# A new layout of SBUF for a fused encoder layer on one core: operands of the large matmuls on the left stack, raw weights and rows on the right

## The chip, the cores and the metric

The kernel runs on one core of a Trainium2 chip. The metric is the device time of one execution in microseconds; for the kernel before it is the median of three runs. The profile is of one further execution, recorded by the hardware profiler.

## The reference, cut to what matters

One layer of an encoder, in float32, for 1024 tokens of width 1024, with 256 memory tokens. Its work is nearly all matrix products:

```
n    = RMSNorm(h)
proj = n @ W_in                         # 1024 x 5120: q,k,v of attention; q,k,v,gate of retention; q of memory
y_a  = dilated windowed attention (12 heads of 64, dilations 1, 4, 16, rotary)
y_r  = bidirectional retention (6 heads, chunks of 128)
y_m  = cross attention into the 256 memory tokens (4 heads of 128)
h    = h + W_out( sum_i sigmoid(n @ W_gate_i + b_i) * (y_i @ W_proj_i) )
u    = DWConv3(RMSNorm(h) @ W_up)       # 1024 x 5632
out  = RMSNorm(h + (silu(a) * b) @ W_down)   # [a | b] = u, width 2816 each
```

## The kernel before

Every large product is done in float32r with both operands split into a high and a low part, x = xh + xl, and three matmuls per block: lh.rh, lh.rl and ll.rh (`mm3`, lines 174 to 177). The order of their operands follows the first argument as the stationary tile of 128 x 128 and the second as the streamed tile of up to 512 columns; in the profile's rows (`acc<-nTh,wh`) the streamed tile stands first. `hilo` (lines 180 and 181) makes the two parts: ScalarE copies the high one, VectorE subtracts it from the source for the low one.

Weights come through `WStream`: SP's queue loads a raw block of 128 x 1024 (`wraw`, three buffers), `hilo` splits it into `wh` and `wl` (three buffers each), TensorE uses it. The order of the loads and splits is written out once, and `get` runs the loads two or more blocks ahead. The program's order sets the order on each engine; a tile's place is given to the next tile of its tag, or to a pool opened later in the same bytes, when its last reader is through.

The stages, in the order of the profile:

- 0 to 780 us: norm and transposes of x into `nTh`, `nTl` (16 tiles of 128 x 1024 in the pool `n_p`), then the projections `acc<-nT,w`, merged by hand with the attentions' own small matmuls. Their q, k, v are tiles of `qk_p` (`qk_tile`, two buffers for each name); the retention's v comes from matmuls of 256 columns whose stationary tile is nT and whose streamed tile is w.
- 780 to 1158 us: for each of three branches the gates (`accg<-nT,w`, evacuated into q, k, v tiles of `qk_p`, six ahead) and the merge `accg<-y,w` (`gemm`). The y rows are loaded into `wraw` buffers and split into `yh`, `yl`; those of k = 0 lie in a pool of their own, `y0_p`. The sum is built in `mg` and split into `mgh`, `mgl`, which take the places of nT.
- 1158 to 1254 us: the output product `pso<-w,mg`, 256 columns, stationary tile mg.
- 1254 to 1325 us: the second norm, and the operands of the up product. That product is done by a scheme with seven products of half size for eight: operands B11, B21 (pool `na_p`) and T2, T1, T3, B22, T4 (pool `nb_p`), each of four tiles for the high and four for the low part, 128 x 512.
- 1325 to 1709 us: the up product over 22 column blocks, seven groups of twelve matmuls each (`prod`), with the convolution on ScalarE and VectorE beside it. The first three column blocks run in the stage before.
- 1709 to 1932 us: the down product `ps<-w,t`, with seven half-size products again, stationary tiles `th`, `tl` made from the rows `g` just before their use.

The pools of SBUF are two stacks: a pool opened without a side lies on the left one, which grows upward, a pool with `side="right"` on the right one, which grows downward from byte 229,344 of a partition. Summed up from the sizes of the pools, the tiles that this document speaks of begin at these bytes; the last column is what the address leaves when divided by 64 (tiles of one pool are 2048 or 4096 bytes long, so it is the same for all of them):

| tiles | before: first byte (side) | remainder |
|---|---|---|
| raw weights; wh; wl | 20,032; 32,320; 44,608 (left) | 0 |
| mh, ml (memory rows, transposed) | 118,304; 126,496 (left, behind small tables) | 32 |
| x | 93,728 (left, behind small tables) | 32 |
| q, k, v of attention, gates | 139,232 to 163,808 (right) | 32 |
| nT, later mgh, mgl | 163,808 to 229,344 (right) | 32 |
| y of k = 0: yh; yl | 131,040; 135,136 (right) | 32 |
| y of k > 0; mg | 89,664 to 130,624; 56,896 (left) | 0 |
| B11; B21 | 114,240; 130,624 (left) | 0 |
| T2, T1, T3, B22, T4 | 147,424 to 229,344 (right) | 32 |
| g of the first four; th, tl | 114,240; 130,624 (left) | 0 |
| the other g | from 147,424 (right) | 32 |

Of the kernel before, what the change touches and what calls it, by code (L numbers as in the profile page):

```python
# [11 lines left out]
F32 = mybir.dt.float32  # L12
F32R = mybir.dt.float32r
# [4 lines left out]
P = 128  # L18
D = 1024
S = 1024  # L20
KT = D // P
NT = S // P
MEM = 256
# [6 lines left out]
HALF = 512  # L30
# [115 lines left out]
def encoder_block(ctx: ExitStack, tc: tile.TileContext, x, mem, vec, w_mix, w_gate, w_pa, w_pr, w_pm,  # L146
# [5 lines left out]
    def pool(name, **kw):  # L152
        kw.setdefault("bufs", 1)
        return tc.tile_pool(name=name, reuse_waits="tile", **kw)
# [28 lines left out]
    class WStream:  # L183

        def __init__(self, wp, raw_bufs=3, bufs=3):
            self.wp, self.raw_bufs, self.bufs = wp, raw_bufs, bufs
            self.loads, self.items, self.raw, self.done = [], [], [], []
            self.i = 0  # L190

# [18 lines left out]
        def _load(self):  # L210
            parts, alt = self.loads[len(self.raw)]
            n = sum(a * b for _, a, b in parts)
            if alt:
                t = self.alt.tile([P, n], F32, name="wraw2", tag="wraw2", bufs=2)
            else:
                t = self.wp.tile([P, n], F32, name="wraw", tag="wraw", bufs=self.raw_bufs)
            at = 0
            for src, a, b in parts:
                nc.sync.dma_start(t[:, at:at + a * b], src.rearrange("p a b -> p (a b)"))
                at += a * b  # L220
            self.raw.append(t)
# [59 lines left out]
        nc.vector.scalar_tensor_tensor(dstl, pt[:, :n], gain[:, k + k0:k + k0 + 1], dsth.bitcast(F32),  # L281
                                       op0=ALU.mult, op1=ALU.subtract)

    W = WStream(ctx.enter_context(pool("w_p")))
    for i, (_, _, nr, _, _) in enumerate(mixer_blocks()):
        W.plain(chunk_spec(w_mix, i, nr // P))
    order = [(1, w_pr, 6), (0, w_pa, 6), (2, w_pm, 4)]
# [15 lines left out]
    NB = DFF // P  # L303
# [73 lines left out]
    down_items()  # L377


    rn = ExitStack()  # L380
    n_p = rn.enter_context(pool("n_p", side="right"))
    nTh = [n_p.tile([P, S], F32R, name=f"nTh{k}", tag="n", bufs=16) for k in range(KT)]
    nTl = [n_p.tile([P, S], F32R, name=f"nTl{k}", tag="n", bufs=16) for k in range(KT)]

    qk_s = ExitStack()
    qk_p = qk_s.enter_context(pool("qk_p", side="right"))
    pm = ExitStack()
    psA = pm.enter_context(pool("psA", space=PS))

# [26 lines left out]
    vmr = [ck.tile([P, 2, HALF], F32R, name="vm" + t, tag="vm" + t) for t in "hl"]  # L416
    xs_ = ExitStack()
    xp = xs_.enter_context(pool("xin"))
    mt = [xp.tile([P, D], F32, name=f"mem{t}", tag="x", bufs=6) for t in range(MEM // P)]
    xt = [xp.tile([P, D], F32, name=f"x{t}", tag="x", bufs=6) for t in range(NT)]  # L420
    for t in range(2):
        nc.sync.dma_start(mt[t], mem[t * P:(t + 1) * P, :])
        if t == 0:
# [124 lines left out]
        return ev  # L548

    def qk_tile(tag, dt=F32):  # L550
        return qk_p.tile([P, S], dt, name=tag, tag=tag, bufs=2)


    def dense_ret_qk(j, st):
# [2 lines left out]
        return [q for p in zip(a, b) for q in p]  # L557

    def dense_ret_v(j, st):
        st["v"] = [qk_p.tile([P, NT, P], F32, name="v0", tag="v", bufs=2),  # L560
                   st["pool"].tile([P, NT, P], F32, name="v1", tag="v1", bufs=2)]
        box = {}

        def vpart(t2):
            if t2 == 0:
                box["w"] = (W.get(), W.get())
            ps = acc()
            for i in range(2):
                t = 2 * t2 + i
                for k in range(KT):  # L570
                    wh, wl = box["w"][k // 4]
                    mm3(ps[:, i * 256:(i + 1) * 256], nTh[k][:, t * P:(t + 1) * P], nTl[k][:, t * P:(t + 1) * P],
                        wh[:, k % 4], wl[:, k % 4], k == 0, k == KT - 1)
            for i in range(2):
                nc.scalar.copy(st["v"][i][:, 2 * t2:2 * t2 + 2, :],
                               ps.rearrange("p (a i b) -> p a i b", a=2, i=2)[:, :, i])

        return [lambda t2=t2: vpart(t2) for t2 in range(4)]
# [411 lines left out]

    def y_part(bi, k):

        r = W.wp.tile([P, S], F32, name="yraw", tag="wraw", bufs=3)
        nc.sync.dma_start(r, y_src[bi][k * P:(k + 1) * P, :])
        a, b = y_tile("yh", k), y_tile("yl", k)
        hilo(a, b, r)
        return a, b

    def y_tile(tag, k):
        if k == 0:  # L1000
            return y0_p.tile([P, S], F32R, name=tag, tag=tag)
        return y_p.tile([P, S], F32R, name=tag, tag=tag, bufs=5)


# [31 lines left out]
    bp_s.close()  # L1036

    sgs = {}
    y0_p = qk_s.enter_context(pool("y0_p", side="right"))
    ap_s = ExitStack()  # L1040
    attn_psum(ap_s, "dil", s=3, t=2, u=1)
    psb["U"] = ap_s.enter_context(pool("dilU"))
# [24 lines left out]
        return psG.tile([P, HALF], F32, name="accg", tag="accg", bufs=8)  # L1067

    gs = ExitStack()
    mg_p = gs.enter_context(pool("mg"))  # L1070
    mg = [mg_p.tile([P, S], F32, name=f"mg{c}", tag="mg", bufs=8) for c in range(KT)]
    y_p = gs.enter_context(pool("y_p"))
    def gemm(w, rh, rl):
# [40 lines left out]
            if bi != 2 and c + GA < KT:  # L1114
                run(gate_steps(bi, c + GA, sgs, accg))
    gs.close()
    qk_s.close()
    pg.close()


# [2 lines left out]
    KP = KT // 2  # L1123
    po = ExitStack()
    psO = po.enter_context(pool("psO", space=PS))
    row_p = ctx.enter_context(pool("row_p"))
    sn_p = ctx.enter_context(pool("sn_p"))
    na_s = ExitStack()
    na_p = na_s.enter_context(pool("na_p"))
    ssq = cst.tile([P, NT, 4], F32, name="ssq")  # L1130
    h_d = dram.tile([S, D], F32, name="h_d")
    g_d = dram.tile([DFF, S], F32, name="g_d")
# [10 lines left out]
    def ops(pl, name):  # L1143
        return [[pl.tile([P, HALF], F32R, name=f"{name}{q}{k}") for q in "hl"] for k in range(KP)]

    B11, B21 = ops(na_p, "b11"), ops(na_p, "b21")
    h_t = {}

    def load_h(ts):
# [194 lines left out]
        conv_q.extend(conv_steps(st["b"], st.pop("ua"), st.pop("ub")))  # L1344

    nb_s = ExitStack()
    nb_p = nb_s.enter_context(pool("nb_p", side="right"))
    T2, T1, T3, B22, T4 = (ops(nb_p, q) for q in ("t2", "t1", "t3", "b22", "t4"))
    w1 = wget()
    pre = []  # L1350
# [68 lines left out]


    NK = NB // 2
    na_s.close()
    t_p = ctx.enter_context(pool("t_p"))
    g_t = []

    def load_g(pl, n):
        for _ in range(n):
            b = len(g_t)
            g_t.append(pl.tile([P, S], F32, name=f"g{b}"))
            nc.gpsimd.dma_start(g_t[b], g_d[b * P:(b + 1) * P, :])  # L1430

    load_g(t_p, 4)
    finish_up(last, *w32, n=(3, 3, 3))
    c12(last)
    nb_s.close()
    gb_p = ctx.enter_context(pool("gb_p", side="right"))
    W.alt = gb_p
    load_g(gb_p, NB - 4 - 2)
    hr = [row(f"hr{t}") for t in range(NT)]
    for t in range(NT):  # L1440
        nc.gpsimd.dma_start(hr[t], h_d[t * P:(t + 1) * P, :])
# [1 line left out]
    nc.gpsimd.dma_start(gfin, bass.AP(tensor=g_final.tensor, offset=g_final.offset, ap=[[0, P], [1, D]]))  # L1443

    def t_op(src):
        h = t_p.tile([P, HALF], F32R, name="th", tag="th", bufs=4)
        l = t_p.tile([P, HALF], F32R, name="tl", tag="tl", bufs=4)
        hilo(h, l, src)
        return h, l

# [71 lines left out]
    for p in range(3):  # L1522
        if p < 2:
            B = [bank() for _ in range(TP)]
        for kp in range(NK):
            w = W.get()
            prep(p * NK + kp + 1)
            if p == 0 and kp == 0:
                fill(len(conv_q))
                load_g(gb_p, 2)  # L1530
            oa, ob = ready.pop((p, kp))
            end = kp == NK - 1
            for tp in range(TP):
                tile_mm(A[tp], tp, oa, w, 0, p == 0 and kp == 0, end)
            if end:
                for tp in range(TP):
                    after_a(p, tp)
            for tp in range(TP):
                tile_mm(B[tp], tp, ob, w, 1, p < 2 and kp == 0, end)
            if end:  # L1540
                for tp in range(TP):
                    after_b(p, tp)
        if p == 0:
            early = [lambda t=t: (square(t, L, 0), gain(t, L)) for t in range(TP)]
        if p == 1:
            run(early)
# [54 lines left out]
```

## Time and profile before

| | |
|---|---|
| median of 3 runs | 1934.61 us (1932.96 to 1935.24) |
| profiled execution | 1934.28 us |
| its span, first to last instruction | 1932.5 us |
| TensorE busy | 1892.1 us, 9458 matmuls |
| VectorE busy | 1142.5 us |
| ScalarE busy | 836.6 us |

A row of the timeline gives the start and the duration of an instruction; matmuls overlap, so the time that one takes from TensorE is the distance to the next one's start. A window gives the busy time of each engine with the number of its instructions, and the granted clock (1.00 is the full 2.4 GHz).

### The profile page before, as it was taken

Reading aid. Unit: us, or ns where it says so; the run is one execution under the profiler, and the core shown is the slowest. Engines: PE = TensorE matmul, PEld = TensorE weight load, DVE = VectorE, ACT = ScalarE, POOL = GpSimd, SP = SyncE. Lnnn points to the kernel's source line nnn. Section 1 sums busy time; section 2 is a strip of 40 time slices with the busy share of each in tenths; the row PEclk is TensorE's granted clock in tenths of the full one; section 3 lists DMA queues with packets and bytes.
Section 4 is the critical chain, followed back from the end, with each engine's and each line's share of the span. In section 5 each row is a group of like instructions: output and inputs, shape, how many; then the busy total and the mean of one; then the engine's idle time right before and its main releaser. Section 6 shows DMA issues by size and latency. Waiting matters only on the chain.

```text
span 1932.5 us, 24176 instructions
## 1 busy us (share of the span) xinstructions
PE 1892.1 (98%) x9458; PEld 1555.5 (80%) x9458; DVE 1142.5 (59%) x2032; ACT 836.6 (43%) x1415; POOL 79.3 (4%) x144
## 2 busy tenths in 40 slices
PE   8999999999999999999999999979999999999997
PEld 7888988887777777788888889957888888888885
DVE  7564454654548526331233074475888887899976
ACT  7364243444556547212112133543545544445444
POOL 1000010110000000000000000000000000020001
PEclk9999999999999999999999999989999999999998
DMA  7211111110011101322112025312222222287552
GB/s 258 88 44 55 44 55 34 55 62 26 23 35 53 44 20 61 109 87 90 34 60 93 22 71 203 114 55 65 77 98 77 94 81 86 75 341 256 170 169 104
DMA packets 52162, 173.35 MB, mean 90 GB/s; under 512 B 6224, under 2 KB 6352, under 8 KB 51920
## 3 DMA queue, kind: packets, MB, share of 16 engines
q1 hardware_dynamic: 39168, 129.33, 20.3%
q0 software_dynamic: 10864, 38.80, 5.1%
q10 hardware_dynamic: 2016, 3.67, 0.5%
q8 instruction: 74, 1.21, 0.3%
q14 instruction: 40, 0.33, 0.1%
HBM read 143.47 MB, written 28.31 MB: 89 GB/s over the span
## 4 chain that ended last, share of the span: by engine, by line
PE 90%; DVE 5%; ACT 3%; issue 1%; DMA 1%; POOL 0%; SPq 0%; POOLq 0%; ACTq 0%; DVEq 0%
PE ps L177 10%; PE ps L176 10%; PE ps L175 10%; PE acc L175 8%; PE acc L177 8%; PE acc L176 8%; PE accg L176 7%; PE accg L177 7%; PE accg L175 7%; PE psu L827 2%; PE pso L177 2%; PE pso L175 2%; PE pso L176 2%; PE pss L783 2%; PE pst L810 1%
## 5 line engine op out<-in xcount | busy, mean ns | idle before, releaser
L181 DVE TENSOR_TENSOR wl<-wraw,wh 128x1024 fp32r<-128x1024 f32 (+2 forms) x239 | 270.8, 1134 | 318.5 <-ACT wh L180 318.5
L180 ACT CAST wh<-wraw 128x1024 fp32r<-128x1024 f32 (+2 forms) x239 | 233.1, 980 | 403.6 <-PE accg L176 170.0
L175 PE MATMUL acc<-nTh,wh 128*128 128x512 f32 x640 | 260.0, 406 | 0.7 <-ACT v L541 0.7
L177 PE MATMUL acc<-nTh,wl 128*128 128x512 f32 x640 | 255.1, 399 | 0.0
L176 PE MATMUL acc<-nTl,wh 128*128 128x512 f32 x640 | 254.5, 398 | 0.0
L175 PEld LDWEIGHTS acc<-nTh,wh 128*128 128x128 f32 x640 | 120.5, 188 | 31.8 <-issue 4.6
L177 PEld LDWEIGHTS acc<-nTh,wl 128*128 128x128 f32 x640 | 120.5, 188 | 28.7 <-issue 1.4
L176 PEld LDWEIGHTS acc<-nTl,wh 128*128 128x128 f32 x640 | 120.7, 189 | 25.5 <-issue 0.7
L176 PE MATMUL ps<-wl,th 128*128 128x512 f32 x308 | 119.8, 389 | 0.0
L175 PE MATMUL ps<-wh,th 128*128 128x512 f32 x308 | 119.8, 389 | 0.0
L177 PE MATMUL ps<-wh,tl 128*128 128x512 f32 x308 | 119.6, 389 | 0.2 <-DVE tl L181 0.2
L177 PE MATMUL accg<-nTh,wl 128*128 128x512 f32 x288 | 114.2, 396 | 0.0
L175 PE MATMUL accg<-nTh,wh 128*128 128x512 f32 x288 | 114.2, 396 | 0.0
L176 PE MATMUL accg<-nTl,wh 128*128 128x512 f32 x288 | 114.2, 396 | 0.0
L529 ACT COPY sw<-acc 32x512 f32<-32x512 f32 x144 | 83.1, 577 | 45.8 <-PE acc L177 39.3
L176 PE MATMUL accg<-yl,wh 128*128 128x512 f32 x256 | 100.4, 392 | 0.0
L175 PE MATMUL accg<-yh,wh 128*128 128x512 f32 x256 | 99.6, 391 | 0.8 <-ACT v L985 0.8
L177 PE MATMUL accg<-yh,wl 128*128 128x512 f32 x256 | 100.3, 392 | 0.0
L180 ACT CAST th<-g 128x512 fp32r<-128x512 f32 x66 | 41.0, 620 | 86.7 <-PE ps L176 70.0
L175 PE MATMUL pso<-wh,mgh 128*128 128x256 f32 x256 | 73.1, 286 | 0.0
L177 PE MATMUL pso<-wh,mgl 128*128 128x256 f32 x256 | 72.5, 283 | 0.0
L176 PE MATMUL pso<-wl,mgh 128*128 128x256 f32 x256 | 71.9, 281 | 0.0
(364 smaller groups left out, 4150.7 us busy)
## 6 DMA issues: line engine op xcount, KB each, us to landing
wraw<-in_w_mlp_dram SPq DMA_DIRECT2D x90, 512.0 KB, 4.1
wraw<-in_w_mix_dram SPq DMA_DIRECT2D x48, 512.0 KB, 3.5
wraw<-in_w_gate_dram SPq DMA_DIRECT2D x24, 512.0 KB, 3.5
g_d<-cv POOLq DMA_DIRECT2D x22, 512.0 KB, 2.9
g<-g_d POOLq DMA_DIRECT2D x22, 512.0 KB, 13.6
wraw<-in_w_out_dram SPq DMA_DIRECT2D x16, 512.0 KB, 3.7
wraw<-in_w_mlp_dram SPq DMA_DIRECT2D x22, 256.0 KB, 3.1
x<-in_x_dram SPq DMA_DIRECT2D x8, 512.0 KB, 5.7
```

Source lines behind the costliest of these rows:

```text
L175: nc.tensor.matmul(o, lh, rh, start=first, stop=False, **kw)
L176: nc.tensor.matmul(o, lh, rl, start=False, stop=False, **kw)
L177: nc.tensor.matmul(o, ll, rh, start=False, stop=last, **kw)
L180: nc.scalar.copy(hi, src)
L181: nc.vector.tensor_sub(lo, src, hi.bitcast(F32))
L529: nc.scalar.copy(sw[q * 32:(q + 1) * 32], ps[o * 32:(o + 1) * 32])
L783: nc.tensor.matmul(ps[:, a * w:(a + 1) * w], st["q"][r, q0:q0 + P], st["k"][r, k0:k0 + w], start=True, stop=True)
L810: nc.tensor.transpose(pv[:, k, a], sm[:, a, k * P:(k + 1) * P], ident)
L827: nc.tensor.matmul(u[64 * i:64 * i + 64, c], loc["V"][:, vslot[k0 + k * P], 64 * i:64 * i + 64], pt[:, k, a], start=k == 0, stop=k == nk - 1)
```

## The change

The allocation of SBUF alone is changed; no engine instruction is added or taken away. The split weights stay on the left and raw weights get a pool `wr_p` on the right. A ring of eight tiles of 128 x 1024, `ab`, follows on the left and serves in turn memory rows and x, q, k and v of all attentions, both v of the retention, gates, y of k = 0, B11 and B21 (high and low part as two halves of one tile), the first four g and th, tl. nT comes behind it on the left, and nb_p and gb_p take its place later. mg, row_p (h, ua, ub, cv and others) and sn_p (half rows) go to the right.

| tiles | after: first byte (side) | remainder |
|---|---|---|
| wh; wl | 20,032; 32,320 (left) | 0 |
| the ring ab | 44,608 to 77,376 (left) | 0 |
| nT, later mgh, mgl | 77,376 to 142,912 (left) | 0 |
| mh, ml | from 187,936 (left, behind small tables) | 32 |
| y of k > 0 | 142,912 to 183,872 (left) | 0 |
| T2, T1, T3, B22, T4 | 77,376 to 159,296 (left) | 0 |
| the other g | from 77,376 (left) | 0 |
| raw weights | 217,056 to 229,344 (right) | 32 |
| mg; row_p; sn_p | 184,288; 167,904; 159,712 (right) | 32 |

```diff
-        def __init__(self, wp, raw_bufs=3, bufs=3):
+        def __init__(self, wp, rp, raw_bufs=3, bufs=3):
...
-                t = self.wp.tile([P, n], F32, name="wraw", tag="wraw", bufs=self.raw_bufs)
+                t = self.rp.tile([P, n], F32, name="wraw", tag="wraw", bufs=self.raw_bufs)
...
-    W = WStream(ctx.enter_context(pool("w_p")))
+    W = WStream(ctx.enter_context(pool("w_p")), ctx.enter_context(pool("wr_p", side="right")))
...
+    ab_p = ctx.enter_context(pool("ab_p"))
+
+    def ab(name, dt=F32, shape=(P, S)):
+        return ab_p.tile(list(shape), dt, name=name, tag="ab", bufs=8)
+
     rn = ExitStack()
-    n_p = rn.enter_context(pool("n_p", side="right"))
+    n_p = rn.enter_context(pool("n_p"))
...
-    qk_s = ExitStack()
-    qk_p = qk_s.enter_context(pool("qk_p", side="right"))
...
-    mt = [xp.tile([P, D], F32, name=f"mem{t}", tag="x", bufs=6) for t in range(MEM // P)]
-    xt = [xp.tile([P, D], F32, name=f"x{t}", tag="x", bufs=6) for t in range(NT)]
+    mt = [ab(f"mem{t}") for t in range(MEM // P)]
+    xt = [ab(f"x{t}") if t < 6 else xp.tile([P, D], F32, name=f"x{t}", tag="x", bufs=2) for t in range(NT)]
...
     def qk_tile(tag, dt=F32):
-        return qk_p.tile([P, S], dt, name=tag, tag=tag, bufs=2)
+        return ab(tag, dt)
...
-        st["v"] = [qk_p.tile([P, NT, P], F32, name="v0", tag="v", bufs=2),
-                   st["pool"].tile([P, NT, P], F32, name="v1", tag="v1", bufs=2)]
+        st["v"] = [ab("v0", shape=(P, NT, P)),
+                   ab("v1", shape=(P, NT, P))]
...
-        r = W.wp.tile([P, S], F32, name="yraw", tag="wraw", bufs=3)
+        r = W.rp.tile([P, S], F32, name="yraw", tag="wraw", bufs=3)
...
         if k == 0:
-            return y0_p.tile([P, S], F32R, name=tag, tag=tag)
+            return ab(tag, F32R)
...
-    y0_p = qk_s.enter_context(pool("y0_p", side="right"))
...
-    mg_p = gs.enter_context(pool("mg"))
+    mg_p = gs.enter_context(pool("mg", side="right"))
...
-    row_p = ctx.enter_context(pool("row_p"))
-    sn_p = ctx.enter_context(pool("sn_p"))
-    na_s = ExitStack()
-    na_p = na_s.enter_context(pool("na_p"))
+    row_p = ctx.enter_context(pool("row_p", side="right"))
+    sn_p = ctx.enter_context(pool("sn_p", side="right"))
...
-    B11, B21 = ops(na_p, "b11"), ops(na_p, "b21")
+    def pair(name):
+        t = ab(name, F32R)
+        return t[:, :HALF], t[:, HALF:]
+
+    B11, B21 = ([pair(f"{q}{k}") for k in range(KP)] for q in ("b11", "b21"))
...
-    nb_p = nb_s.enter_context(pool("nb_p", side="right"))
+    nb_p = nb_s.enter_context(pool("nb_p"))
...
-            g_t.append(pl.tile([P, S], F32, name=f"g{b}"))
+            g_t.append(ab(f"g{b}") if b < 4 else gb_p.tile([P, S], F32, name=f"g{b}"))
...
-    gb_p = ctx.enter_context(pool("gb_p", side="right"))
+    gb_p = ctx.enter_context(pool("gb_p"))
...
-        h = t_p.tile([P, HALF], F32R, name="th", tag="th", bufs=4)
-        l = t_p.tile([P, HALF], F32R, name="tl", tag="tl", bufs=4)
+        h, l = pair("th")
```

## Rows read from the trace of the kernel before

**Rows 1.** The page: the span.
```profile
span 1932.5 us, 24176 instructions
```

**Rows 2.** The page, chain that ended last: shares of the span by engine.
```profile
PE 90%; DVE 5%; ACT 3%; issue 1%; DMA 1%; POOL 0%; SPq 0%; POOLq 0%; ACTq 0%; DVEq 0%
```

**Rows 3.** Windows: length, then busy us (instructions) by engine, clock, DMA share, GB/s.
```profile
10.00:20.00 10.00, 9.76 (x69) 9.43 (x69) 9.02 (x24) 9.90 (x26) 1.65 (x3) 1.00 0.91 351
100.00:780.00 680.00, 674.47 (x3707) 547.93 (x3706) 363.71 (x941) 331.33 (x658) 27.84 (x48) 1.00 0.14 45
780.00:1158.00 378.00, 377.99 (x1631) 306.30 (x1630) 117.02 (x148) 84.81 (x108) 0.00 (x0) 1.00 0.22 68
1158.00:1254.00 96.00, 96.00 (x800) 95.57 (x799) 44.91 (x82) 42.98 (x96) 7.95 (x14) 1.00 0.45 159
1254.00:1325.00 71.00, 58.94 (x237) 44.23 (x237) 47.63 (x76) 28.99 (x48) 1.24 (x2) 0.88 0.16 57
1325.00:1709.00 384.00, 382.92 (x1648) 309.50 (x1647) 313.88 (x344) 190.04 (x227) 16.95 (x32) 1.00 0.27 90
```

**Rows 4.** Timeline of TensorE, gate matmuls: start us, us, instruction.
```profile
900.06 0.39 PE L175 MATMUL accg<-nTh,wh 128*128 128x512 f32 x1
...
903.57 0.39 PE L175 MATMUL accg<-nTh,wh 128*128 128x512 f32 x1
```

**Rows 5.** Timeline of TensorE, one merge sum from its first matmul (k = 0) on.
```profile
818.99 0.39 PE L175 MATMUL accg<-yh,wh 128*128 128x512 f32 x1
...
820.39 0.39 PE L175 MATMUL accg<-yh,wh 128*128 128x512 f32 x1
...
821.76 0.39 PE L175 MATMUL accg<-yh,wh 128*128 128x512 f32 x1
...
825.84 0.39 PE L175 MATMUL accg<-yh,wh 128*128 128x512 f32 x1
```

**Rows 6.** Timeline of TensorE, up product: B21, then T4, then T2.
```profile
1400.21 0.39 PE L175 MATMUL ps<-b21h,wh 128*128 128x512 f32 x1
...
1402.93 0.40 PE L175 MATMUL ps<-t4h,wh 128*128 128x512 f32 x1
...
1405.74 0.40 PE L175 MATMUL ps<-t2h,wh 128*128 128x512 f32 x1
```

**Rows 7.** Tiles acc, accg, pso, ps: duration ns min/median/max, first and last start, forms.
```profile
L175 PE MATMUL acc<-nTh,wh x640: 387/397/506, 32.0 to 778.0; 128*128 128x512 f32 x160
L175 PE MATMUL acc<-wh,nTh x192: 277/282/369, 143.9 to 304.2; 128*128 128x256 f32 x192
L175 PE MATMUL accg<-nTh,wh x288: 392/397/401, 781.6 to 1113.5; 128*128 128x512 f32 x144
L177 PE MATMUL accg<-yh,wl x256: 387/389/400, 780.2 to 1158.2; 128*128 128x512 f32 x128
L175 PE MATMUL pso<-wh,mgh x256: 279/285/369, 1158.4 to 1254.1; 128*128 128x256 f32 x128
L175 PE MATMUL ps<-t3h,wh x88: 394/398/400, 1295.0 to 1706.2; 128*128 128x512 f32 x88
```

**Rows 8.** Timeline of TensorE, stationary tile mh, streamed tile wh.
```profile
48.66 0.40 PE L175 MATMUL pss<-wh,mh 128*128 128x512 f32 x1
...
51.23 0.39 PE L177 MATMUL pss<-wh,ml 128*128 128x512 f32 x1
```

**Rows 9.** VectorE: the tile tl (min/median/max); raw weights, by form (busy us, mean ns).
```profile
L181 DVE TENSOR_TENSOR tl<-g,th x66: 675/684/694, 1702.7 to 1911.2; 128x512 fp32r<-128x512 f32 x66
...
L181 DVE TENSOR_TENSOR wl<-wraw,wh 128x1024 fp32r<-128x1024 f32 x192 | 234.4, 1222 | 231.8 <-ACT wh L180 231.8
```

**Rows 10.** DMA issues: count, KB each, median us from issue to landing.
```profile
x<-in_x_dram SPq DMA_DIRECT2D x8, 512.0 KB, 5.7
h<-in_x_dram SPq DMA_DIRECT2D x8, 512.0 KB, 6.1
```

**Rows 11.** Timeline of SP's queue where the rows h are loaded.
```profile
1162.05 2.43 SPq L1152 DMA_DIRECT2D h<-in_x_dram  x5
```

More of the change, by code (lines that the diff above doesn't have):

```diff
@@ L183, in encoder_block @@
     class WStream:
-        def __init__(self, wp, raw_bufs=3, bufs=3):
-            self.wp, self.raw_bufs, self.bufs = wp, raw_bufs, bufs
+        def __init__(self, wp, rp, raw_bufs=3, bufs=3):
+            self.wp, self.rp, self.raw_bufs, self.bufs = wp, rp, raw_bufs, bufs
             self.loads, self.items, self.raw, self.done = [], [], [], []
@@ L1116, in encoder_block @@
     gs.close()
-    qk_s.close()
     pg.close()
@@ L1421, in encoder_block, with load_g @@
     NK = NB // 2
-    na_s.close()
-    t_p = ctx.enter_context(pool("t_p"))
     g_t = []
-    def load_g(pl, n):
+    def load_g(n):
         for _ in range(n):
             b = len(g_t)
-            g_t.append(pl.tile([P, S], F32, name=f"g{b}"))
+            g_t.append(ab(f"g{b}") if b < 4 else gb_p.tile([P, S], F32, name=f"g{b}"))
             nc.gpsimd.dma_start(g_t[b], g_d[b * P:(b + 1) * P, :])
-    load_g(t_p, 4)
+    load_g(4)
     finish_up(last, *w32, n=(3, 3, 3))
@@ L1435, in encoder_block @@
     nb_s.close()
-    gb_p = ctx.enter_context(pool("gb_p", side="right"))
+    gb_p = ctx.enter_context(pool("gb_p"))
     W.alt = gb_p
-    load_g(gb_p, NB - 4 - 2)
+    load_g(NB - 4 - 2)
     hr = [row(f"hr{t}") for t in range(NT)]
@@ L1529, in encoder_block @@
                 fill(len(conv_q))
-                load_g(gb_p, 2)
+                load_g(2)
             oa, ob = ready.pop((p, kp))
```

## The prediction, made before the changed kernel was run

> **What bounds the kernel now.** I read the page first: the span is 1932.5 us [rows 1], and the chain of work that ended last is 90% TensorE [rows 2]. The windows by stage then show where this holds [rows 3]: between 780 and 1254 us and between 1325 and 1709 us TensorE has no idle time worth the name, between 100 and 780 us it lacks 5.5 us of 680, and only the stretch 1254 to 1325 us (59 of 71 us busy) and the tail wait for others. The granted clock is 1.00, the 2.4 GHz level, in all the full stretches. So what TensorE needs for one matmul is what the kernel costs, and since matmuls are pipelined I read it as the distance from start to start, not as the duration.
>
> These distances fall into two classes, although all the matmuls compared are float32r with 512 columns at the same clock. Gate matmuls that stream nT: 900.06 to 903.57 us, 15 steps, 234.0 ns each [rows 4]. Merge matmuls that stream y: 821.76 to 825.84 us, 18 steps, 226.7 ns [rows 5]. In one row of the up product the class changes in mid-stream without any wait: twelve steps on B21 take 2.72 us (226.7 ns), the twelve on T4 behind them 2.81 us (234.2 ns) [rows 6]. The median durations say the same for whole tiles: 397 ns for nT, 398 for T3, 389 for y [rows 7].
>
> The layout table ahead of this explains the classes. Every slow operand (nT, T1 to T4, B22, the y tiles of k = 0) starts at a byte that leaves 32 when divided by 64; every fast one (y of k > 0, B11, B21) leaves 0, and so do the split weights wh and wl, which meet both. The y tiles of k = 0 decide between this and "high addresses are slow": they lie at 131,040, inside the span of the fast B21 (130,624 to 147,008), and from 818.99 to 820.39 us their six steps take 233.3 ns each [rows 5]. The next six, already on tiles with remainder 0, take 228.3 before the distance settles at 226.7. It is not the streamed operand alone: where the stationary tile is mh (remainder 32) and the streamed one wh (remainder 0), 11 steps take 2.57 us, 233.6 ns [rows 8].
>
> **The change part by part.** It moves nT, the up operands, y of k = 0 and the q, k, v tiles to the left stack, where every pool ahead of them is a multiple of 64 bytes long: the split weights at 20,032, the ring of eight at 44,608, nT at 77,376, y at 142,912, all with remainder 0. Raw weights, merge sums, rows and the normalised rows go right, to remainder 32.
>
> (1) nT streamed: 3 x 640 projection and 3 x 288 gate matmuls [rows 7] = 2784, each 234.0 - 226.7 = 7.3 ns less: 20.3 us. TensorE is the bound in both stages [rows 3]; the 5.5 us it lacks in the first may grow a little, so I count 95% of the projection part (1920 x 7.3 = 14.0) and all of the gates': 19.6 us.
>
> (2) Up operands: 15 operands' worth of 88 matmuls (T3 as one of them [rows 7]) = 1320. Those of the first three column blocks run where TensorE waits for ScalarE and VectorE, and are worth nothing; in 1325 to 1709 us run 1648 matmuls [rows 3], five of seven groups of them on these operands: 1177 x 7.5 ns = 8.8 us.
>
> (3) y of k = 0: 3 rounds x 8 columns x 2 halves x 3 = 144 matmuls x 7 ns = 1.0 us, and the six steps behind each of the 24 merges' k = 0, now 1.6 ns late, 0.2 us; I take as much again for B11, which runs behind B22. Together 1.4 us.
>
> (4) Matmuls of 256 columns with a stationary operand at remainder 32: 768 in the output product, 576 for the retention's v [rows 7]. The former, with 32 transposes among them, are 800 in 96.0 us, 120.0 ns each [rows 3]; no row shows one with both operands at remainder 0. Bounds: nothing gained, should something other than the operands' reading set those 120 ns, and half of a fast 512-column step, 113.4 ns, so 6.6 ns or 8.9 us in all; a loss I exclude, since no row shows remainder 0 slower than 32. The stationary mh cost a 512-column matmul 6.9 ns [rows 8], nearly what a streamed operand costs, which is nearer the upper end: I take 5 ns, 6.7 us.
>
> (5) Raw weights go to remainder 32, the only heavily read tiles that get worse. For VectorE the subtraction for t reads g tiles of both kinds (four of 22 at 0, the others at 32), and all 66 lie between 675 and 694 ns; the same operation of 1024 columns on raw weights takes 1.22 us [rows 9]. For the DMA queue, 512 KB landed in 5.7 us on the x tiles (remainder 32) and in 6.1 us on h (remainder 0) [rows 10]. I cost it at nothing; what hides a small loss is the slack of VectorE (314 of 384 us busy in the up product [rows 3]) and three raw buffers.
>
> (6) Waits. The ring of eight takes over the tiles of several pools. I counted what lives at a time: eight rows of memory and x at the start, eight at the retention's change of head pair (two times q, k, v0, v1), eight from the sixth gate on (six gates, two y tiles), four B11 and four B21, four g and four t. Each new tile finds one whose last reader stands earlier in the program, so no wait is added; in the retention two bufs per name become any of eight, which loosens. The rows x have ten places for ten tiles instead of six, so their loads go out at once; ScalarE is busy for 9.9 of 10 us there [rows 3] and sets that stretch, so I cost this at nothing either. The rows h now lie over y tiles, free only when the last merge matmul has run at 1158.2 us [rows 7], but their loads leave SP's queue at 1162.05 us, behind raw weights [rows 11]: covered by 3.8 us. Behind them in the queue only further raw weights wait. Zero.
>
> (7) The attention's small fp32 matmuls on q, k and v go from remainder 32 to 0 with one operand: some 480 passes. They stand between waits of their own chains, and no row compares them; between 0 and 7 ns each, 0 to 3.4 us, I take 0.
>
> Sum: 19.6 + 8.8 + 1.4 + 6.7 = 36.5 us. Against the profiled execution's own time, 1934.28 us (1.8 us outside its span), that gives 1897.8; the median of the runs shown is 0.3 us above that execution, so **1898 us**.
>
> A rule of the Trainium skill speaks against all this. "TensorE: Matmul & The Clock Gate", section Back-to-back issue gap, gives the distance as N/2.4 + 2.5 ns, 215.8 ns for 512 columns, with no term for an address; the rows show 226.7 and 234. "SBUF — State Buffer", section Specifications, puts lines at 16 bytes, by which a start with remainder 32 is as good as one with 0. By both the sum would be 0; the sharp change within [rows 6] disagrees, and no sentence above needs them.
>
> **The rivals.** *No change (5%)*: the classes come from something that travels with the tile but not with its place, such as which engine wrote it or the group it accumulates in. For: I see two classes, not their cause. Against: B21 and T4 are written by the same pair of engines and accumulate twelve deep alike, y changes class between k = 0 and k = 2 of one sum. Then 1932 to 1938 us.
>
> *The region counts, not the remainder (8%)*: slow above some 143,000 bytes. nT, T1 to T3 and B22 come to lie below 142,912, T4 and y of k > 0 above. Gain: 19.6, four fifths of 8.8 = 7.0, 1.0 and 6.7; loss: 768 - 144 = 624 merge matmuls x 7.3 = 4.6. Sum 29.7 us: 1905, and 1911 if (4) brings nothing. Against it stand the y tiles of k = 0.
>
> *Slower (4%)*: raw weights at remainder 32 slow VectorE. In the up product a column block is 84 matmuls, 19.4 us, with VectorE busy for 82% of it [rows 3], 15.9 us, of which 7.1 us read raw weights (three splits of 1.22, one of half the width and four sums of that width at the 0.69 us of t). When these 7.1 us grow by the 3.5 us of slack, half again, VectorE sets the pace; the gains outside this stage, 28 us, are eaten by another 1.5 us in each of 19 blocks, so it decides from 70% on. Doubled it gives 1935 - 28 + 19 x 3.6 = 1975 us. Against it stand the 66 rows of t [rows 9].
>
> **How the numbers follow.** The forecast's case has 83%: within it (4) may give 0 to 8.9, (7) up to 3.4, (1) 0.7 and (2) 1.1 more if the parts I left out profit too: 1934.6 less 29.8 to 43.9, 1891 to 1905. The region's case reaches 1911. I state 1890 to 1911; outside lie no change, slower, and the main case where a wait I have not seen takes more than 6 us, together under 2 in 10. A measurement of this kernel tells about 0.2% (4 us) from no change: faster 0.91 (main and region), same 0.05, slower 0.04.
>
> **What would show it.** In the profile after: gate matmuls 226 to 228 ns apart and 389 ns long instead of 397; T3 and T4 389; about 441 matmuls in a full 100 us of the up product; the output product's 256-column steps at 113 to 116 ns if (4) is right, 120 if not; merge matmuls on k > 0 unchanged at 226.7, and all steps of k = 0 with them; VectorE's subtraction on raw weights still 1.22 us; the down product (1709 to 1932 us, remainder 0 before and after) as long as now. Wrong would be: gates still at 234 (no change), y of k > 0 or T4 at 234 (region), idle time of TensorE put down to VectorE's wl (slower), or to q, k, v or y tiles (the ring holds too few).

## The result, and the profile after

The changed kernel took 1916.8 to 1921.0 us where the kernel before took 1933.78 us: a ratio of 0.9925, interval 0.9905 to 0.9944. Measured again (four runs, median 1916.35 us, against 1932.94 us) the ratio was 0.9913 [0.9899, 0.9928]. Forecast were 1898 us and a range from 1890 to 1911: the sign came as said, but less than half of the gain. One execution of the changed kernel, the one profiled with these, took 4787.62 us, with its 512-column matmuls 595 ns apart for a reason that its record does not show, so the rows here are from the second measurement, whose profiled execution took 1915.63 us.

The tiles of TensorE, against [rows 7] (duration in ns, then first and last start in us):

```profile
L175 PE MATMUL acc<-nTh,wh x640: 387/389/628, 38.4 to 777.4; 128*128 128x512 f32 x160
...
L175 PE MATMUL accg<-nTh,wh x288: 387/389/395, 780.6 to 1105.9; 128*128 128x512 f32 x144
...
L177 PE MATMUL accg<-yh,wl x256: 387/389/398, 779.6 to 1149.9; 128*128 128x512 f32 x128
...
L175 PE MATMUL pso<-wh,mgh x256: 277/283/366, 1150.1 to 1245.8; 128*128 128x256 f32 x128
...
L175 PE MATMUL ps<-t3h,wh x88: 389/389/394, 1286.4 to 1688.2; 128*128 128x512 f32 x88
```

The streamed tiles that took 397 or 398 ns in [rows 7] are at 389 now. The gates, against [rows 4], and the up product, against [rows 6]:

```profile
893.10 0.39 PE L175 MATMUL accg<-nTh,wh 128*128 128x512 f32 x1
...
896.50 0.39 PE L175 MATMUL accg<-nTh,wh 128*128 128x512 f32 x1
...
1392.41 0.39 PE L175 MATMUL ps<-t4h,wh 128*128 128x512 f32 x1
...
1395.13 0.39 PE L175 MATMUL ps<-t2h,wh 128*128 128x512 f32 x1
```

Fifteen gate steps take 3.40 us and the twelve on T4 2.72 us: 226.7 ns each, where they were 234.0 and 234.2. So the matmuls became as fast as forecast, and the time went elsewhere. The starts in the tile rows cut the span into four parts; the gains add up to the difference of the spans, 1932.5 - 1913.9 = 18.6 us. The forecast's terms are put where their matmuls stand; the 6.7 us of term (4) are 2.9 for the retention's v and 3.8 for the output product:

| part | before [rows 7] | after | gain | forecast |
|---|---|---|---|---|
| to the first merge matmul (`yh,wl`) | 780.2 | 779.6 | 0.6 | 16.2 |
| gates and merges | 378.0 | 370.3 | 7.7 | 7.5 |
| output product | 95.7 | 95.7 | 0.0 | 3.8 |
| from its end to the span's end | 678.4 | 668.1 | 10.3 | 9.0 |

Two parts are nearly right, the output product with its 256 columns gained nothing, and the part with the projections, which hold the largest term, gained 0.6 us. The windows of after show two places in them where TensorE now has less to do: at the start, against the first of [rows 3], and near 610 us:

```profile
10.00:20.00 10.00, 9.18 (x70) 8.66 (x70) 9.05 (x25) 9.98 (x26) 1.65 (x3) 1.00 1.03 414
20.00:30.00 10.00, 9.03 (x71) 7.86 (x69) 8.76 (x23) 9.69 (x22) 3.30 (x5) 1.00 0.87 340
30.00:40.00 10.00, 8.21 (x55) 6.73 (x55) 9.95 (x18) 8.72 (x18) 0.00 (x0) 1.00 0.29 87
...
605.00:610.00 5.00, 4.54 (x21) 3.41 (x19) 5.00 (x7) 3.10 (x6) 0.00 (x0) 1.00 0.00 2
610.00:615.00 5.00, 0.74 (x2) 0.30 (x2) 5.00 (x11) 0.49 (x2) 1.62 (x3) 0.76 0.26 98
615.00:620.00 5.00, 4.96 (x14) 3.32 (x15) 5.00 (x18) 2.54 (x11) 0.00 (x0) 0.56 0.15 59
```

TensorE runs two matmuls between 610 and 615 us, and while it waits the granted clock falls to the 1.2 GHz level (mean 0.76 in these 5 us, 0.56 in the next 5). The timeline of the place:

```profile
610.21 0.50 PE L175 MATMUL acc<-nTh,wh 128*128 128x512 f32 x1 [0.68 <-ACT v L545]
610.55 0.40 PE L176 MATMUL acc<-nTl,wh 128*128 128x512 f32 x1
615.04 2.07 PE L787 MATMUL pss<-k,q 64*128 64x256 f32 x4 [4.09 <-DVE nm L793]
617.04 1.11 PE L814 MATMUL pst<-ident,sm 128*128 128x128 f32 x4
```

and the same place in the kernel before:

```profile
613.71 0.51 PE L175 MATMUL acc<-nTh,wh 128*128 128x512 f32 x1 [0.68 <-ACT v L541]
614.05 0.39 PE L176 MATMUL acc<-nTl,wh 128*128 128x512 f32 x1
...
617.56 0.40 PE L176 MATMUL acc<-nTl,wh 128*128 128x512 f32 x1
618.04 1.13 PE L783 MATMUL pss<-k,q 64*128 64x256 f32 x4
```

There the scores `pss<-k,q` stand behind 17 matmuls of a projection's second half, which cover the time that VectorE needs; after the change they stand behind two, and the other 15 come later in TensorE's order, so they wait with them. VectorE is busy for all of the 5 us in both kernels; the window of before:

```profile
610.00:615.00 5.00, 4.33 (x19) 3.16 (x19) 5.00 (x6) 1.53 (x3) 0.00 (x0) 1.00 0.00 0
```

No line of the diff moves an instruction, and ahead of the prediction it says that the program's order sets the order on each engine. The traces show that this is not enough: compared matmul by matmul, TensorE's order departs from that of before at the start (26 to 45 us), from 614 to 642 us, and in single places from 736 us on. I take it that the order is planned from when tiles come free, so that one ring for q, k and v gives another plan; the experiments on the order test this.

### The profile page after: what moved, and what is told of

The parts are those of the page before. It is cut to its first block, busy times and chain, and to the rows that moved or that the text cites. A ratio compares the mean times of both kernels' runs of the same rounds, so it can differ in the third digit from the quotient of the medians.

```text
span 4785.8 us, 24106 instructions
## 1 busy us (share of the span) xinstructions
PE 4753.0 (99%) x9458; PEld 3038.4 (63%) x9458; DVE 1160.9 (24%) x2032; ACT 842.3 (18%) x1415; POOL 78.9 (2%) x144
## 4 chain that ended last, share of the span: by engine, by line
PE 99%; DVE 0%; DMA 0%; ACT 0%; issue 0%; SPq 0%; POOLq 0%; POOL 0%; ACTq 0%
PE ps L176 11%; PE ps L177 11%; PE ps L175 11%; PE acc L175 9%; PE acc L177 9%; PE acc L176 9%; PE accg L175 7%; PE accg L176 7%; PE accg L177 7%; PE psu L831 2%; PE pss L787 2%; PE pso L176 2%; PE pso L175 2%; PE pso L177 2%; PE pst L814 1%; PE psy L684 1%
## 5 line engine op out<-in xcount | busy, mean ns | idle before, releaser
L175 PE MATMUL acc<-nTh,wh 128*128 128x512 f32 x640 | 535.7, 837 | 0.7 <-ACT v L545 0.7
L177 PE MATMUL acc<-nTh,wl 128*128 128x512 f32 x640 | 533.3, 833 | 0.0
L176 PE MATMUL acc<-nTl,wh 128*128 128x512 f32 x640 | 528.9, 826 | 0.0
L175 PE MATMUL ps<-wh,th 128*128 128x512 f32 x308 | 255.1, 828 | 0.0
L176 PE MATMUL ps<-wl,th 128*128 128x512 f32 x308 | 255.0, 828 | 0.0
L177 PE MATMUL ps<-wh,th 128*128 128x512 f32 x308 | 255.0, 828 | 0.0
L177 PE MATMUL accg<-nTh,wl 128*128 128x512 f32 x288 | 238.6, 828 | 0.0
L176 PE MATMUL accg<-nTl,wh 128*128 128x512 f32 x288 | 238.3, 828 | 0.0
L177 PEld LDWEIGHTS ps<-wh,th 128*128 128x128 f32 x308 | 108.4, 352 | 75.1 <-issue 75.1
L175 PEld LDWEIGHTS ps<-wh,th 128*128 128x128 f32 x308 | 108.4, 352 | 75.1 <-issue 73.7
L175 PE MATMUL ps<-b,wh 128*128 128x512 f32 x176 | 146.4, 832 | 0.0
L177 PE MATMUL ps<-b,wl 128*128 128x512 f32 x176 | 146.2, 830 | 0.0
```

What stands on the lines that cost most here:

```text
L175: nc.tensor.matmul(o, lh, rh, start=first, stop=False, **kw)
L176: nc.tensor.matmul(o, lh, rl, start=False, stop=False, **kw)
L177: nc.tensor.matmul(o, ll, rh, start=False, stop=last, **kw)
```

## The experiments

Each was timed beside runs of the kernel before, whose median lay between 1932.4 and 1932.9 us.

**The remainder alone.** The kernel before with one small tile opened first on the right, and, beside it, the changed kernel again:

```diff
+    pad_p = ctx.enter_context(pool("pad_p", side="right"))
+    nc.gpsimd.memset(pad_p.tile([P, 8], F32, name="pad"), 0.0)
```

> The kernel before with one tile of 32 bytes opened first on the right-hand side, so that nT, q, k, v, y of k = 0 and the up operands move down by 32 bytes and leave 0 divided by 64, with every region, ring and wait as before. Remainder theory: gates 226.7 ns apart, up product 226.7, 30 to 36 us less than before (ratio 0.981 to 0.985). Region theory: nothing changes, ratio 1.000, gates at 234.

> The changed kernel once more, for a profile whose clock can be compared with that of before. Remainder theory (a matmul is slower when an operand's first byte leaves 32 divided by 64): gate matmuls 226.7 ns from start to start instead of 234.0, T1 to T4 and B22 226.7, y of all k 226.7; then the 36 us forecast must have been lost again elsewhere, as idle time or low clock of TensorE, some 22 us of it. Region theory (slow above some 143,000 bytes): nT and T1 to T3 226.7, T4 and y of k > 0 at 234. Third theory (the distance depends on the pair of operands): gates between 226.7 and 234, with no idle time added.

The pad gave 1927.09 us, ratio 0.9971 [0.9960, 0.9981], and the changed kernel 1916.35. The gates of the padded kernel:

```profile
893.47 0.39 PE L175 MATMUL accg<-nTh,wh 128*128 128x512 f32 x1
893.70 0.40 PE L176 MATMUL accg<-nTl,wh 128*128 128x512 f32 x1
893.94 0.39 PE L177 MATMUL accg<-nTh,wl 128*128 128x512 f32 x1
894.17 0.40 PE L175 MATMUL accg<-nTh,wh 128*128 128x512 f32 x1
...
898.14 0.39 PE L177 MATMUL accg<-nTh,wl 128*128 128x512 f32 x1
```

From 893.47 to 898.14 us are 20 steps of 233.5 ns on average, now some 229 and 237 ns in turn. The starts of both operands of these matmuls leave 0 when divided by 64 here, so the remainder by 64 is not what makes a matmul fast. The merges on y of k > 0, which nothing moved, stayed at 227 ns. What differs between them is how far the streamed and the stationary tile stand apart: a multiple of 512 bytes for y of k > 0 and for all of the changed kernel's large operands, 416 bytes more for nT before (163,808 - 32,320 is 256 x 512 + 416), 384 more with the pad. (The stationary tile is a slice of 512 bytes of the weight, so which slice it is changes nothing in this.) Neither expectation came true: the pad gained 5.9 us, not 30 to 36 and not nothing. At 384 bytes the projections' steps are 232.5 ns on average where they were 234.0, and the gates' 233.2 where they were 234.2.

**A map of distances outside the layer.** Series of 48 matmuls on two tiles, without the layer.

> Leaves out the whole layer. After 8 rows of x are loaded it runs series of 48 float32r matmuls on one 128x128 stationary and one 512-column streamed tile; stationary and streamed start are the same modulo 4096 bytes in the first series, then the streamed start is shifted by 32 to 480 bytes (mov), the stationary one (sta), or both by the same amount (both); further ones shift the streamed start by 512 to 8192 bytes (far), or take 256 and 128 columns (half, quar). Theory A, the distance depends on the difference of the two starts: all 15 of 'both' at 226.7 ns, those of 'mov' and 'sta' mostly 233 to 234 ns, with one or a few shifts fast and the rest slow, 'far' fast at multiples of the period. Theory B, each operand's own start counts modulo 64: fast exactly where every shift is a multiple of 64, slow at odd multiples of 32, in 'mov', 'sta' and 'both' alike. Theory C, each operand's own start counts modulo something larger (128 to 512): 'both' is slow as 'mov' is. 256 columns: 120 ns at any shift if the floor lies elsewhere.

It tells nothing of the addresses. The distances were 595 ns in the first 25 series and 465 to 468 in the next ones with 512 columns, whatever the shift, 234 with 256 and with 128 columns alike:

```profile
600.00:700.00 100.00, 100.00 (x170) 59.14 (x169) 0.00 (x0) 1.76 (x3) 0.00 (x0) 1.00 0.00 0
800.00:900.00 100.00, 100.00 (x215) 63.41 (x214) 0.00 (x0) 2.34 (x4) 0.00 (x0) 1.00 0.00 0
```

170 matmuls in 100 us are not what the layer shows elsewhere, but the layer's own 512-column matmuls stood the same 595 ns apart when it took 4787.62 us. So these distances do not come from leaving out the layer. The granted clock of 1.00 explains nothing here, since the traces of these two executions hold no event of the clock at all. The cause stays open, and the question went back into the layer.

**Equal starts without the new layout.** The kernel before, with nT, T1 to T4, B22 and y of k = 0 moved by 416 bytes:

```diff
+    rt_p = ctx.enter_context(pool("rt_p", side="right"))
+    small = rt_p.tile([P, 104], F32, name="small")
...
-    lg = com.tile([P, 18], F32, name="lg")
+    lg = small[:, :18]
...
-    na, zz, acc_ = (sm18(f"ls{i}") for i in range(3))
+    na, zz, acc_ = (small[:, a:a + 18] for a in (18, 36, 54))
```

> The kernel before with a tile of 416 bytes opened first on the right-hand side, so that nT, T1 to T4, B22 and y of k = 0 start at the same byte modulo 4096 as the split weights (four small tables of 72 bytes move into it); order of all instructions, x loads and everything else as before. Theory A (the difference of the two operands' starts counts): gates and nT projections at 226.7 ns, so 3 x 640 + 3 x 288 nT matmuls and about 1177 in the up product gain 7 ns each, 1903 to 1907 us in all, and nothing is lost at the start or at 610 us: first nT matmul at 31.9 us, no wait of TensorE there. Theory B (remainder by 64, what the 32-byte pad tried): no better than that pad, about 1927 us, gates at 232 ns. Rival D (TensorE's projections are paced by something else, the shorter distance is given back in waits): first gate still near 779 us although the distances are 226.7, 1915 to 1920 us.

1907.85 us, ratio 0.9868 [0.9854, 0.9883], just above the 1903 to 1907 of theory A: one tile of 416 bytes gains more than the whole new layout. All 9458 matmuls stand in the order of before, so the order has no part in this gain.

```profile
L175 PE MATMUL acc<-nTh,wh x640: 387/389/507, 32.7 to 769.0; 128*128 128x512 f32 x160
...
L175 PE MATMUL accg<-nTh,wh x288: 389/389/396, 772.6 to 1097.2; 128*128 128x512 f32 x144
...
L177 PE MATMUL accg<-yh,wl x256: 388/389/397, 771.2 to 1141.2; 128*128 128x512 f32 x128
...
L175 PE MATMUL pso<-wh,mgh x256: 277/283/364, 1141.4 to 1237.0; 128*128 128x256 f32 x128
```

In the four parts of the table above it gains 9.0, 8.0, 0.1 and 9.8 us, together 26.9 (span 1905.6). So the operands are worth 9.0 us in the projections, not 13.3. The reason stands in the timeline behind one group of small matmuls:

```profile
426.25 1.14 PE L782 MATMUL pss<-k,q 64*128 64x256 f32 x8
427.32 0.50 PE L175 MATMUL acc<-nTh,wh 128*128 128x512 f32 x1
427.67 0.40 PE L176 MATMUL acc<-nTl,wh 128*128 128x512 f32 x1
427.90 0.40 PE L177 MATMUL acc<-nTh,wl 128*128 128x512 f32 x1
...
429.99 0.39 PE L177 MATMUL acc<-nTh,wl 128*128 128x512 f32 x1
...
431.12 0.39 PE L176 MATMUL acc<-nTl,wh 128*128 128x512 f32 x1
```

From 427.67 to 429.99 us ten steps take 232 ns each, from 429.99 to 431.12 five take 226: the short distance settles only some ten matmuls behind a group of another kind. Over all groups the first three projection matmuls behind an interruption are 232 ns apart, the eleventh and later 226.7. The attentions' small matmuls break the projections up into 127 groups. With the order the same, the two traces can be set against each other matmul by matmul: 1699 of the 1920 steps lead straight to the next projection matmul, and they went from 234.0 to 228.2 ns on average, 9.9 us in all; the 221 steps at the edges of the groups gained nothing; 0.8 us went with a later first projection (32.7 against 32.0 us).

**The difference or each start by itself.** The changed kernel with its start and its order of before (`after_tags_six`, below), and all its left-hand tiles shifted together:

```diff
+    sh_p = ctx.enter_context(pool("sh_p"))
+    nc.gpsimd.memset(sh_p.tile([P, 40], F32, name="shift"), 0.0)
     W = WStream(ctx.enter_context(pool("w_p")), ctx.enter_context(pool("wr_p", side="right")))
```

> after_tags_six with a tile of 160 bytes opened first on the left stack: split weights, ring, nT, y, T1 to T4, B22, th and tl all begin 160 bytes later, at remainder 32 by 64 (224 by 512), and stand to each other as before. Raw weights, mg and rows stay. The order of instructions is the same. Theory A (the difference of the two operands' starts counts): nothing changes, gates stay 226.7 ns apart, 1906 to 1910 us. Theory B (each operand's own start, by 64 or by any larger power of two up to 512): all the large matmuls slow, gates at 234 ns, more than 5000 matmuls at 5 to 7 ns, 1935 us or more.

1906.92 us, ratio 0.9863 [0.9846, 0.9879], the gates still at 389 ns:

```profile
L175 PE MATMUL accg<-nTh,wh x288: 389/389/397, 772.6 to 1097.5; 128*128 128x512 f32 x144
```

With all starts at remainder 32 by 64 nothing got slower. As far as this shift can show, it is the difference of the two starts that counts, not where either stands.

**How far apart.** Ten of the 16 nT tiles 32 bytes longer:

```diff
-    nTh = [n_p.tile([P, S], F32R, name=f"nTh{k}", tag="n", bufs=16) for k in range(KT)]
...
+    def n_tile(q, k):
+        i = k + KT * (q[-1] == "l")
+        return n_p.tile([P, S + (8 if i < 10 else 0)], F32R, name=f"{q}{k}", tag=f"n{i}")[:, :S]
```

> after_tags_six with the first ten nT tiles 32 bytes longer, so that the streamed tile begins 0, 32, 64, ... 288 bytes (nTh0 to nTh7, nTl0, nTl1) and 320 bytes (nTl2 to nTl7) behind the stationary one modulo 512; the weights stay. Read from the 96 gate matmuls on each pair of nT tile and weight. Theory A with only equal starts fast: nTh0 at 226.7 ns, all others 232 to 234. Theory A with a shorter period: nTh0 and nTh4 and nTl0 fast for 128, nTh0 and nTl0 for 256, every second one for 64. The 32-byte pad (a difference of 384) was slow by 6 ns, which speaks against 64 and 128. The time lies between 1908 and 1933 us, near 1928 if only one tile of 16 is fast.

```profile
L175 PE MATMUL accg<-nTh,wh x288: 388/395/399, 778.2 to 1109.1; 128*128 128x512 f32 x144
...
L176 PE MATMUL accg<-yl,wh x256: 387/388/502, 776.6 to 1153.5; 128*128 128x512 f32 x128
L177 PE MATMUL accg<-yh,wl x256: 388/392/401, 776.8 to 1153.7; 128*128 128x512 f32 x128
```

1915.64 us in one execution, in which TensorE's order at the start differs too. The reading by tile failed: the gates were 232.2 ns apart on average, and nTh0, with a difference of 0, 230 like its neighbours. This would fit the settling seen behind small matmuls, if among others of other differences a matmul has no settled distance; it is not shown. The y of k > 0 came to lie 320 bytes off, all of them alike, and were 232, 227 and 230 ns apart in turn. Every difference met that is no multiple of 512 bytes (32 for the stationary mh in [rows 8], 320, 384, 416, and the mixture) gives 230 to 234 ns on average. A period of 128 bytes or less is excluded by 384; whether 256 bytes would do is not shown, since the tile that had them stood in the mixture.

**The order near 610 us.** The changed kernel, its ring cut into four names of two places; the bytes stay:

```diff
-    def ab(name, dt=F32, shape=(P, S)):
-        return ab_p.tile(list(shape), dt, name=name, tag="ab", bufs=8)
+    turn = [0]
+
+    def ab(name, dt=F32, shape=(P, S), tag=None, of="qkvw"):
+        if tag is None:
+            tag = of[turn[0] % len(of)]
+            turn[0] += 1
+        return ab_p.tile(list(shape), dt, name=name, tag="ab" + tag, bufs=2)
...
-        return ab(tag, dt)
+        return ab(tag, dt, tag=tag)
```

> The changed kernel with its ring of eight cut into four names of two places each, the bytes unchanged: q, k, v and the second v of the retention have two places each as before the change, all other tiles go round the four names in turn, which gives them the places of the ring. The order of TensorE's instructions is then that of the kernel before from the first attention on; the start (x loads at once) stays that of the changed kernel. If the order near 610 us is what costs there (the first score matmul of the next head pair put 15 matmuls earlier, ahead of the work that covers it): the 4 us wait of TensorE for VectorE near 610 us and the half clock behind it are gone, 7 to 8 us less than the changed kernel, 1908 to 1910 us, and the first nT matmul stays at 38.7 us. Rival: the wait comes from the faster matmuls themselves (TensorE overtakes VectorE), then it stays and the time is 1915 to 1918 us.

1910.84 us, ratio 0.9886 [0.9869, 0.9902]: 5.5 us less than the changed kernel, where 7 to 8 were expected. From the first attention to the output product TensorE's order is that of the kernel before. The wait is down from 4.09 us to 0.68, the clock stays:

```profile
615.45 1.13 PE L792 MATMUL pss<-k,q 64*128 64x256 f32 x4 [0.68 <-DVE nm L798]
```

```profile
610.00:615.00 5.00, 4.15 (x17) 3.11 (x17) 5.00 (x9) 0.57 (x1) 1.62 (x3) 1.00 0.18 69
615.00:620.00 5.00, 4.55 (x21) 3.34 (x21) 5.00 (x18) 3.04 (x8) 0.00 (x0) 1.00 0.23 88
```

The first merge matmul starts at 775.2 us instead of 779.6, 4.4 us earlier. The rival that the faster matmuls themselves run into VectorE falls: they are as fast here.

**The start.** The same with memory rows and x in six places, as before the change:

```diff
-    mt = [ab(f"mem{t}") for t in range(MEM // P)]
-    xt = [ab(f"x{t}") if t < 6 else xp.tile([P, D], F32, name=f"x{t}", tag="x", bufs=2) for t in range(NT)]
+    mt = [ab(f"mem{t}", of="qkv") for t in range(MEM // P)]
+    xt = [ab(f"x{t}", of="qkv") for t in range(NT)]
```

> As after_tags, and memory rows and x go round three names, six places, as before the change: x4 to x7 are loaded only when a place is free, and TensorE's order is that of the kernel before at the start too. If the ten places at the start cost the 6.8 us: first nT matmul back at 31 to 33 us, x landing in about 6 us, 6 to 7 us less than after_tags, 1901 to 1904 us. Rival: the later start is made up for later (the wait would have fallen elsewhere), then within 2 us of after_tags. Rival 2: raw weights' place or the new order of other loads delays the start, then the first nT matmul stays near 38 us.

1907.83 us, ratio 0.9868 [0.9854, 0.9883]: 3.0 us less again, half of what was expected. The first projection is back at 32.8 us, but most of the 6 us by which it came late had been used for other work; what was lost is TensorE's idle time between 10 and 40 us. The windows of that stretch, first the kernel before, then the changed one, then this one:

```profile
10.00:40.00 30.00, 29.31 (x208) 26.74 (x207) 27.92 (x62) 28.08 (x62) 5.48 (x8) 1.00 0.76 285
```

```profile
10.00:40.00 30.00, 26.42 (x192) 23.25 (x192) 27.75 (x63) 28.39 (x64) 4.94 (x8) 1.00 0.73 280
```

```profile
10.00:40.00 30.00, 29.55 (x209) 27.39 (x209) 27.79 (x61) 27.95 (x61) 5.48 (x8) 1.00 0.76 285
```

The idle time is 0.7, 3.6 and 0.45 us. On VectorE the splits of raw weights in that stretch have moved, in the changed kernel and in this one:

```profile
33.51 1.21 DVE L181 TENSOR_TENSOR wl<-wraw,wh 128x1024 fp32r<-128x1024 f32 x1
36.43 1.21 DVE L181 TENSOR_TENSOR wl<-wraw,wh 128x1024 fp32r<-128x1024 f32 x1
```

```profile
26.00 1.22 DVE L181 TENSOR_TENSOR wl<-wraw,wh 128x1024 fp32r<-128x1024 f32 x1
29.06 1.22 DVE L181 TENSOR_TENSOR wl<-wraw,wh 128x1024 fp32r<-128x1024 f32 x1
```

With all rows there early, their normalisation and transposes stand ahead of the splits on VectorE. That TensorE then has too little to multiply, and waits while VectorE evacuates transposes, is how I read it; the waits themselves are many and under 1 us each.

**Loads or order at the start.** `after_tags`, ten places, but the last four loads of x written later:

```diff
+        for t in {0: (4, 5), 1: (6, 7)}.get(h, ()):
+            nc.sync.dma_start(xt[t], x[t * P:(t + 1) * P, :])
         dg = [norm_of(xp, xt[t], nc.vector) for t in ts]
```

> after_tags with the loads of x4 and x5 written behind the first memory key block and those of x6 and x7 behind the second; all ten rows keep places of their own, so no load waits for a place. In SP's queue x6 and x7 then stand behind one raw weight block instead of ahead of three, and the transposes of x4 to x7 come later in TensorE's order, about where they are in the kernel before. If the order (TensorE's transposes of x4 to x7 standing ahead of work that is ready, x6 and x7 ahead of the raw weights) costs at the start: first nT matmul near 33 us, time near 1908 us, 3 us less than after_tags. If it is that ten rows share the DMA engines at once: the first nT matmul stays near 38 us and the time near 1911 us.

1910.50 us, ratio 0.9885 [0.9871, 0.9900]: no gain over `after_tags`, and TensorE is busy for 26.59 of the same 30 us. The first projection starts at 35.7 us, between the 33 and the 38 that the two readings expected. This does not decide it. The rows still shared the DMA engines (share 1.03 between 10 and 20 us, x landing after 10.1 us, 9.9 in the changed kernel, 5.7 before [rows 10]), but the splits did not return to their places either (26.3 and 38.1 us), so order and loads are not told apart. Shown is that six places for the rows bring back 3.0 us and later loads do not.

## Why the prediction was wrong, point by point

- *The classes and their sizes* were right: 226.7 ns for nT, T1 to T4, B22 and y of k = 0 in after, durations 389. The cause named for them was not. Remainder 0 by 64 gave 233.5 ns (the 32-byte pad) and remainder 32 gave 226.7 (all shifted by 160): every pair at 226.7 ns has starts that differ by a multiple of 512 bytes. The table ahead of the prediction could not tell the two causes apart, since 32 and 0 went with 416 and 0; [rows 8] fit both, with a difference of 32. That the new layout hit 226.7 ns was luck: its pools on the left happen to lie multiples of 512 bytes apart, which the rule in the prediction did not ask for.
- *The region rival* fell: y of k > 0 and T4 lie from 142,912 bytes upwards in after and run at 226.7 ns. *No change* fell too. *Slower through raw weights*: VectorE's split still takes 1.22 us at its new place, so term (5) was right.
- *Term (1), nT*: the gates' part came (gates and merges 7.7 us against 7.5, (3) with it). The projections' part was mis-sized at 13.3 us: with the order kept this part of the span gains 9.0 us. Of 1920 x 7.3 = 14.0 us, 1.6 fall to the 221 steps at the edges of groups, which gain nothing, some 2.5 to the steps behind each group that have not settled yet, and 0.8 to the later first projection. [rows 5] showed the settling, six steps at 228.3 behind k = 0, and it was used for term (3) alone.
- *Term (2), up operands*: 9.0 us forecast with B11's share, 9.8 us (`pad_416`) and 10.3 us (after) measured for all behind the output product. This part varies by 2 to 3 us between executions: it gained 12.7 us in `after_tags`, where the granted clock of the first 71 us behind the output product was 0.90 on average, against 0.88 in before, after and `pad_416`.
- *Term (4), 256 columns* brought 0 of 6.7 us: the output product takes 95.6 to 95.7 us in before, after and `pad_416`, and the retention's v steps 122 ns on average before and after. Equal starts are not even best there: it takes 95.3 us with the 32-byte pad and 94.4 with the mixture of differences. The lower of the two bounds was the right one.
- *Term (6), waits*, is the step that failed worst: it was put at zero, and up to the first merge after is 8.4 us behind `pad_416` (779.6 against 771.2). "Which loosens" was read as harmless, but with the ring the order came out another way, and scores put ahead of their cover cost 4.4 us up to the first merge. "I cost this at nothing either", of x in ten places, cost 3.0 us. The other 1.0 us is not traced.

The sum, as measured: 26.9 us from the operands (`pad_416`, of its span) less 4.4 near 610 us and 3.0 at the start leaves 19.5, against 18.6 between the spans of before and after; the 0.9 us left is not traced. By the medians the operands are worth 24.5 us (1932.39 - 1907.85), since the profiled execution of before took 1.9 us more than its median and that of `pad_416` 0.5 us less. With both orders put back, `after_tags_six` takes 1907.83 us, the same as the 416-byte pad alone.

## What to carry to other kernels

When the matmul distance of one kernel falls into classes, look at the two operands' starts as a pair before moving pools: here one spacer of 416 bytes did what the new layout was to do, without touching the order. A layout change in a program whose order is planned is also a change of order: compare the engines' instruction order before reckoning that a looser ring costs nothing. And a gain per matmul read from a long uninterrupted stream holds for such streams only: here the steps at the edges of each group gained nothing, and up to ten behind them gained less.

## What the runs showed of the hardware that was not expected

- The distance of float32r matmuls of 512 columns depends on the difference of the streamed and the stationary start: 226.7 ns at multiples of 512 bytes, 234 at 32 and at 416, 233.5 at 384, 230 at 320. A shift of both by 160 bytes changes nothing. With 256 columns nothing is gained: 95.7 us for the output product at 416 and at 0.
- The short distance has to settle: 232 ns in the first steps behind a small matmul, 226.7 from the eleventh on. It is nearly the same sequence each time, entered earlier or later (behind the group shown above: 240, 235, 233, 236, 224, 231, 236, 228, 232, 231, then 227 and 226; elsewhere only its last three or four steps are there).
- In a wait of 4.09 us without matmuls the granted clock fell to 0.5, for some 7 us in all (by the two windows, 5 x 0.24 / 0.5 + 5 x 0.44 / 0.5) and nearly doubled the cost of what stood there (four score matmuls 2.07 us, 1.13 before).
- A program of nothing but matmuls ran them 595 and 465 ns apart for 1400 us. Its windows show a granted clock of 1.00, but its trace holds no event of the clock. The Trainium skill warns in "TensorE: Matmul & The Clock Gate", section Seeing it yourself, that the recorded events of the clock gate have been unreliable on trn2; no run here shows whether that is the reason.
